# Some of the weights' low parts move from VectorE to GpSimd in stretches with urgent chains

## The chip, the cores and the metric

The kernel runs on one core of one Trainium2 chip. The metric is the device time of one execution in microseconds (us), as the median of three runs. Engines are named as the profile names them: PE is TensorE (PEld its weight loads), DVE is VectorE, ACT is ScalarE, POOL is GpSimd, SP is the engine whose queue issues most of the DMAs.

## The reference

The input is one sequence of 256 tokens of width 1024 in float32, with a memory of 256 rows. Two blocks follow each other, each of depth 2:

- Block 1, per layer: rms norm, one projection to 5120 columns (`w_in`), three branches of width 512 (attention of 8 heads with rotary positions over one causal block of 256, a gated linear recurrence called hgrn, attention to the memory), each branch times `silu(z)`, then `w_out` and the residual sum.
- Block 2, per layer: a mixer and a feed-forward net. The mixer projects to retention, a gated delta rule (names `dn`), a pooling branch and three sets of 1024 gates; `y = sum of sigmoid(gate) * (branch @ w_branch)`, then `x = x + rms_norm(y @ w_out)`. The net is `x = x + rms_norm((silu(h @ gate) * (h @ up)) @ down)` with 2816 hidden columns.

All weights are float32 and each is used once per execution.

## The kernel before

**Products.** A float32 product is made of three matmuls in the fp32r type: with x = xh + xl and w = wh + wl, `mm3` (and `chan`) does xh·wh + xh·wl + xl·wh. So each weight tile must be split before use. The weights are cut into units of 256 rows x 512 columns, stored as one tile of 128 x 1024. A unit goes through three steps, all in the class `Stream`: `_dma` loads it into a `raw` tile (5 buffers), `_split_h` casts it to `wh` on ACT, `_split_l` makes `wl = raw - wh` on DVE. The `raw` buffer comes free, for the load of five units later, when `wh` and `wl` are done. Up to 6 (wh, wl) pairs stand in pool `w`, two more in `k4` for units marked as spare.

**Use.** The 256 tokens are two tiles of 128 (t = 0, 1). `tok` takes a unit while t = 0 is worked on, with 6 matmuls for each unit and t, and uses the same units again for t = 1. `out_proj` does the last units for t = 0 and then for t = 1, so that the chain that follows t = 0 (residual, norm, transposes, next `aTh`/`aTl`) runs while PE does t = 1, and the chain of t = 1 runs while PE does t = 0 of the next phase.

**Order.** The program is written by a planner. `Order` keeps an estimated time for PE (`o.pe`) and one for each engine (`_at`; for GpSimd `Engine(self, nc.gpsimd, 150.0, 2.2)`, so 150 ns and 2.2 ns for each element of a row). Work outside the matmuls is generators (tasks) that are polled after every three matmuls; a task continues when what it waits for is ready by the estimate. Tasks spawned with `first=True` are urgent and counted in `o.urgent`: the chains at the ends of phases (`post_norm`, `residual` with the next `norm`), `branch_evac` for the `dn` branch, and the last part of the feed-forward net. At every poll `pump` may do one `_split_l`, loads, and one `_split_h`. While urgent tasks exist, a split is done only if fewer than `LEAST` = 2 split units stand ahead of the one to be taken next, or if `_room` says that the engine will be free again by 300 ns after the next urgent step is due. After the planner, the framework's scheduler orders each engine's instructions by readiness and program order in its own model; so an instruction can slip ahead of one written before it that is not ready. All of DVE's, ACT's and POOL's instructions carry line 109 (the planner's wrapper), so they are told apart by their tiles.

**Names in the rows.** `raw`, `wh`, `wl` as above; `aTh`, `aTl`: high and low part of transposed activations; `sig`, `y`: gate and sum of `branch_evac` (`sig = ps * sig`, then `y = y + sig`); `yg`, `b`, `c`, `v`, `w`, `z`, `r`, `x`, `xn`: the steps of `post_norm` and `norm` (`x = yg * r + x`, `xn = x * r * gain`); `mx`, `acc`: PSUM tiles; `rope...`, `hgrn_masks`, `lbd`, `lbe`: small work of the start.

Of the kernel before, what the change touches and what calls it, by code (L numbers as in the profile page):

```python
# [8 lines left out]
F32 = mybir.dt.float32  # L9
# [5 lines left out]
ALU = mybir.AluOpType  # L15
# [215 lines left out]
class Stream:  # L231
# [66 lines left out]
        m, k = self.units[i][3]  # L298
        return self.kb.mem_gain[m][:, 2 * k : 2 * k + 2]

    def _split_l(self):
        i = self.n_l
        w = math.prod(self.shape(i)[1:])
        h = self.h[i][:, :w]
        gain = self.gain(i)
        if gain is None:
            self.o.dve.tensor_tensor(self.l[i][:, :w], self.raw[i][:, :w], h.bitcast(F32), op=ALU.subtract)
        else:
            for k in range(2):
                c = slice(k * w // 2, (k + 1) * w // 2)  # L310
                self.o.dve.scalar_tensor_tensor(self.l[i][:, c], self.raw[i][:, c], gain[:, k : k + 1], h[:, c].bitcast(F32),
                                                op0=ALU.mult, op1=ALU.subtract)
        del self.raw[i]
        self.n_l += 1
# [9 lines left out]
    def pump(self):  # L324
        o = self.o
        if (self.n_l < self.n_h and o.when(self.h[self.n_l]) <= o.pe + o.SLACK
                and (self.n_l - self.at < self.LEAST or self._room(o.dve, 1140.0))):
            self._split_l()
        while self.n_dma < len(self.units) and self.n_dma - self.n_l < self.RAW:
            self._dma()  # L330
        least = self.n_h - self.at < self.LEAST
        if (self.n_h < min(self.n_dma, self.at + self.AHEAD) and self._can_place()
                and o.when(self.raw[self.n_h]) <= o.pe + (o.SLACK if least else -self.LANDED)
                and (least or self._room(o.act, 960.0))):
            self._split_h()
# [1574 lines left out]
```

## Time and profile before

| | |
|---|---|
| median of three runs | 1415.68 us (1414.83 to 1417.45) |
| the profiled execution's own time | 1415.08 us |
| its span, first to last instruction | 1413.3 us |
| granted clock of TensorE, mean | 0.999 |
| instructions | 20451 |
| busy: PE, PEld, DVE, ACT, POOL | 1386.1, 1166.4, 1017.3, 829.5, 26.1 us |
| DMA: bytes, mean rate | 229.06 MB, 162 GB/s |

PE's ends are modelled and its matmuls overlap, so a busy PE says only that a matmul was in work. POOL's 26.1 us lie in the first two of forty slices of the span; it does nothing after that.

### The profile page before, as it was taken

To read this page: it belongs to the slowest core of one execution; us is meant where nothing else is said; L and a number is where in the kernel's file an instruction comes from. 1 tells how busy PE (TensorE), PEld (TensorE's weight loads), DVE (VectorE), ACT (ScalarE), POOL (GpSimd) and SP (SyncE) were. 2 spreads that over 40 slices of the span, in tenths; PEclk is the share of its full clock that TensorE was granted. 3 is DMA by queue.
4 is the path that set the end of the run, shared out by engine and by line. 5 is a ranking of instruction groups with operands and counts; after the bars stand their busy time and mean duration, and the time that the engine had idled before them with its cause. 6 is when DMAs were issued, how large, how long until landed. Compare 5 with 4: busy or idle time off the path is not lost.

```text
span 1413.3 us, 20451 instructions
## 1 busy us (share of the span) xinstructions
PE 1386.1 (98%) x7608; PEld 1166.4 (83%) x7608; DVE 1017.3 (72%) x1712; ACT 829.5 (59%) x1420; POOL 26.1 (2%) x65
## 2 busy tenths in 40 slices
PE   7999999999999999999999999999999999999998
PEld 6978887887888898888877888879888887788886
DVE  6798677689897698657777655687968567665564
ACT  6676565476764466556655544565666466555453
POOL 6100000000000000000000000000000000000000
PEclk9999999999999999999999999999999999999999
DMA  8653446555345454235665566645534357465561
GB/s 279 205 162 93 136 134 213 170 152 164 120 149 177 123 184 137 80 90 178 214 190 166 190 193 190 213 138 175 150 116 123 96 187 253 120 202 185 182 189 62
DMA packets 123412, 229.06 MB, mean 162 GB/s; under 512 B 10656, under 2 KB 16560, under 8 KB 123312
## 3 DMA queue, kind: packets, MB, share of 16 engines
q1 hardware_dynamic: 123280, 227.75, 51.7%
q8 instruction: 60, 0.98, 0.3%
q14 instruction: 40, 0.33, 0.1%
q0 software_dynamic: 32, 0.00, 0.0%
HBM read 226.67 MB, written 1.05 MB: 161 GB/s over the span
## 4 chain that ended last, share of the span: by engine, by line
PE 83%; DVE 6%; DMA 4%; ACT 3%; issue 3%; SPq 0%; DVEq 0%; ACTq 0%
PE acc L137 57%; PE mx L137 22%; PE mx L147 5%; DVE wl L109 2%; ACT wh L109 2%; DMA raw<-in_w_out 1%; DMA raw<-in_ffn_gate 1%; ACT junk L109 1%; DMA mem<-in_mem 0%; DVE hlf L109 0%; DMA gqk<-in_moba_q_norm 0%; DVE hA L109 0%; ACT sg L109 0%; DMA raw<-in_w_in 0%; SPq L408 0%
## 5 line engine op out<-in xcount | busy, mean ns | idle before, releaser
L109 DVE TENSOR_TENSOR wl<-raw,wh 128x1024 fp32r<-128x1024 f32 x396 | 479.9, 1221 | 148.4 <-ACT wh L109 142.9
L109 ACT CAST wh<-raw 128x1024 fp32r<-128x1024 f32 x396 | 412.7, 1050 | 173.6 <-PE acc L137 93.6
L137 PE MATMUL acc<-wh,aTh 128*128 128x512 f32 x1232 | 494.4, 402 | 2.4 <-ACT aTh L109 2.2
L137 PE MATMUL acc<-wh,aTl 128*128 128x512 f32 x1232 | 485.0, 394 | 1.1 <-DVE aTl L109 1.1
L137 PE MATMUL acc<-wl,aTh 128*128 128x512 f32 x1232 | 485.1, 394 | 0.0
L137 PEld LDWEIGHTS acc<-wh,aTl 128*128 128x128 f32 x1232 | 232.0, 188 | 49.8 <-DVE aTl L109 2.3
L137 PEld LDWEIGHTS acc<-wh,aTh 128*128 128x128 f32 x1232 | 232.3, 189 | 49.2 <-ACT aTh L109 4.1
L137 PEld LDWEIGHTS acc<-wl,aTh 128*128 128x128 f32 x1232 | 232.3, 189 | 45.0 <-issue 1.0
L137 PE MATMUL mx<-wh,ff 128*128 128x512 f32 x352 | 111.2, 392 | 0.0
L137 PE MATMUL acc<-aTh,wh 128*128 128x256 f32 x320 | 91.1, 285 | 0.0
L137 PE MATMUL acc<-aTh,wl 128*128 128x256 f32 x320 | 90.6, 283 | 0.0
L137 PE MATMUL acc<-aTl,wh 128*128 128x256 f32 x320 | 90.5, 283 | 0.0
L137 PEld LDWEIGHTS mx<-wh,ff 128*128 128x128 f32 x352 | 65.6, 188 | 13.2
L109 ACT ACTIVATE sg<-sg 128x512 f32<-128x512 f32 (+1 forms) x120 | 73.7, 614 | 1.5
L109 ACT ACTIVATE sg<-zc 128x512 f32<-128x512 f32 (+1 forms) x60 | 36.9, 616 | 62.4 <-DVE zc L109 62.3
L137 PE MATMUL mx<-wl,ff 128*128 128x512 f32 x176 | 68.5, 389 | 0.0
L137 PEld LDWEIGHTS acc<-aTh,wh 128*128 128x128 f32 x320 | 61.3, 192 | 0.3
L137 PEld LDWEIGHTS acc<-aTh,wl 128*128 128x128 f32 x320 | 61.3, 192 | 0.2
L137 PEld LDWEIGHTS acc<-aTl,wh 128*128 128x128 f32 x320 | 61.3, 192 | 0.0
L109 DVE TENSOR_SCALAR zc<-acc 128x512 f32<-128x512 f32 (+1 forms) x48 | 31.9, 664 | 36.8 <-PE acc L137 36.8
L109 ACT CAST ff<-mx 128x256 fp32r<-128x256 f32 x44 | 14.4, 375 | 52.8 <-PE mx L147 52.8
L109 ACT CAST aTh<-mx 128x512 fp32r<-128x512 f32 x44 | 24.7, 584 | 33.2 <-PE mx L147 32.9
(317 smaller groups left out, 1654.1 us busy)
## 6 DMA issues: line engine op xcount, KB each, us to landing
raw<-in_w_in SPq DMA_DIRECT2D x200, 512.0 KB
raw<-in_ffn_down SPq DMA_DIRECT2D x44, 512.0 KB
raw<-in_w_out SPq DMA_DIRECT2D x40, 512.0 KB
raw<-in_ffn_gate SPq DMA_DIRECT2D x40, 512.0 KB
raw<-in_ffn_up SPq DMA_DIRECT2D x40, 512.0 KB
raw<-in_w_mem_kv SPq DMA_DIRECT2D x16, 512.0 KB
raw<-in_w_branch_pool SPq DMA_DIRECT2D x8, 512.0 KB
raw<-in_w_branch_ret SPq DMA_DIRECT2D x8, 512.0 KB
```

The lines of the kernel that those rows point to most:

```text
L109: r = f(out, *args, **kw)
L137: self._ns.matmul(out, lhsT, rhs, **kw)
L147: self._ns.transpose(out, x, ident)
```

## The change

When `pump` finds a low part to be made whose high part is ready, but neither fewer than two split units ahead nor room on DVE, it did nothing for that unit. Now it gives that `wl` to GpSimd, if there are urgent tasks and GpSimd's estimated time is not past PE's by more than 200 ns. The instruction is the same (`tensor_tensor`, subtract, 128 x 1024). The splits forced in `take`, those with fewer than two units ahead, and those with room stay on DVE; units with a gain never go to GpSimd, since that branch of `_split_l` doesn't use the new argument.

```diff
-    def _split_l(self):
+    def _split_l(self, engine=None):
         i = self.n_l
         w = math.prod(self.shape(i)[1:])
         h = self.h[i][:, :w]
         gain = self.gain(i)
         if gain is None:
-            self.o.dve.tensor_tensor(self.l[i][:, :w], self.raw[i][:, :w], h.bitcast(F32), op=ALU.subtract)
+            (engine or self.o.dve).tensor_tensor(self.l[i][:, :w], self.raw[i][:, :w], h.bitcast(F32), op=ALU.subtract)
...
         if (self.n_l < self.n_h and o.when(self.h[self.n_l]) <= o.pe + o.SLACK
                 and (self.n_l - self.at < self.LEAST or self._room(o.dve, 1140.0))):
             self._split_l()
+        elif self.n_l < self.n_h and o.urgent and o.when(self.h[self.n_l]) <= o.pe + o.SLACK and o.gps._at <= o.pe + o.SLACK:
+            self._split_l(o.gps)
         while self.n_dma < len(self.units) and self.n_dma - self.n_l < self.RAW:
             self._dma()
```

## Rows read from the trace of the kernel before

**Rows 1.** The page's busy times: us, share of the span, instructions.
```profile
PE 1386.1 (98%) x7608; PEld 1166.4 (83%) x7608; DVE 1017.3 (72%) x1712; ACT 829.5 (59%) x1420; POOL 26.1 (2%) x65
```

**Rows 2.** Windows: stretch, length, busy time of PE, PEld, DVE, ACT, POOL, clock, DMA.
```profile
703.40:721.30 17.90, 15.42 (x73) 11.67 (x72) 15.19 (x19) 8.91 (x12) 0.00 (x0) 1.00 0.80 259
727.00:739.00 12.00, 12.00 (x58) 9.87 (x58) 9.94 (x21) 9.46 (x20) 0.00 (x0) 1.00 0.50 138
739.00:753.00 14.00, 13.30 (x64) 10.56 (x63) 12.45 (x27) 7.27 (x17) 0.00 (x0) 1.00 0.55 183
...
917.00:932.00 15.00, 13.21 (x60) 10.11 (x59) 13.04 (x27) 12.13 (x26) 0.00 (x0) 1.00 0.53 161
...
1183.20:1201.20 18.00, 15.22 (x73) 11.62 (x72) 15.36 (x19) 9.08 (x12) 0.00 (x0) 1.00 0.85 288
...
1219.00:1233.00 14.00, 13.32 (x64) 10.57 (x63) 12.45 (x27) 7.18 (x17) 0.00 (x0) 1.00 0.57 184
...
sum 166.80, PE 158.37 PEld 126.28 DVE 140.36 ACT 93.26 POOL 0.00; mean PE 11.31 PEld 9.02 DVE 10.03 ACT 6.66 POOL 0.00
```

**Rows 3.** The same 14 windows, instructions on tile wl alone (PE, PEld, DVE).
```profile
244.00:253.00 9.00, 4.61 (x13) 2.26 (x12) 3.46 (x3) 1.00 0.40 112
...
1386.00:1396.00 10.00, 5.44 (x15) 2.64 (x14) 2.36 (x2) 1.00 0.00 0
sum 166.80, PE 79.36 PEld 38.33 DVE 58.70; mean PE 5.67 PEld 2.74 DVE 4.19
```

**Rows 4.** Timeline of DVE after the first `dn` product: start, us, instruction.
```profile
704.83 1.21 DVE L109 TENSOR_TENSOR wl<-raw,wh 128x1024 fp32r<-128x1024 f32 x1
705.96 0.68 DVE L109 TENSOR_TENSOR y<-y,sig 128x512 f32<-128x512 f32 x1
```

**Rows 5.** Timeline of PE there; in brackets idle before it and its releaser.
```profile
705.00 0.39 PE L137 MATMUL acc<-wl,aTh 128*128 128x512 f32 x1
705.23 0.39 PE L137 MATMUL acc<-wh,aTl 128*128 128x512 f32 x1
...
706.79 0.63 PE L147 MATMUL mx<-ident,y 128*128 128x128 f32 x4 [0.95 <-DVE y L109]
```

**Rows 6.** Timelines of DVE and PE in the chain behind mixer 0, t = 1.
```profile
743.71 1.21 DVE L109 TENSOR_TENSOR wl<-raw,wh 128x1024 fp32r<-128x1024 f32 x1
744.84 0.15 DVE L109 SCALAR_TENSOR_TENSOR r<-w,z 128x1 f32<-128x1 f32 x1
...
750.62 1.23 PE L147 MATMUL mx<-ident,xn 128*128 128x128 f32 x8 [0.62 <-DVE xn L109]
```

**Rows 7.** Timeline of DVE in the chain behind the first feed-forward net, t = 0.
```profile
925.25 1.23 DVE L109 TENSOR_TENSOR wl<-raw,wh 128x1024 fp32r<-128x1024 f32 x1
926.39 0.15 DVE L109 SCALAR_TENSOR_TENSOR r<-w,z 128x1 f32<-128x1 f32 x1
```

**Rows 8.** Timeline of POOL and DVE at the start.
```profile
9.99 0.25 POOL L109 TENSOR_TENSOR ropea<-ropea,ropez 128x32 f32<-128x32 f32 x1
...
10.47 1.22 DVE L109 TENSOR_TENSOR wl<-raw,wh 128x1024 fp32r<-128x1024 f32 x1 [0.58 <-ACT wh L109]
10.70 1.10 POOL L109 TENSOR_TENSOR ropea<-ropea,ropez 128x32 f32<-128x32 f32 x1
```

**Rows 9.** Timeline of POOL and DVE around a cast of masks.
```profile
48.28 1.23 DVE L109 TENSOR_TENSOR wl<-raw,wh 128x1024 fp32r<-128x1024 f32 x1 [0.22 <-ACT wh L109]
48.78 1.20 POOL L109 CAST hgrn_masks<-stage 128x512 uint8<-128x512 f32 x1 [0.46 <-DMA stage<-in_c_hgrn_masks]
...
49.64 0.35 DVE L109 TENSOR_TENSOR lbd<-cols 128x4 f32<-128x4 f32 x1
...
50.16 0.15 DVE L109 SCALAR_TENSOR_TENSOR lbe<-lbd 128x4 f32<-128x4 f32 x1
```

**Rows 10.** Groups by form on DVE, 703.4 to 753: busy us, mean ns, idle before.
```profile
L109 DVE SCALAR_TENSOR_TENSOR x<-yg,r,x 128x512 f32<-128x512 f32 x4 | 2.8, 749 | 0.1
L109 DVE SCALAR_TENSOR_TENSOR xn<-x,r,gain 128x512 f32<-128x512 f32 x4 | 2.8, 748 | 0.0
...
L109 DVE TENSOR_TENSOR y<-y,sig 128x512 f32<-128x512 f32 x4 | 2.7, 680 | 0.0
```

## The prediction

> **What bounds the kernel now.** I read the page first. PE is in work for 1386.1 of 1413.3 us [rows 1]; DVE is busy for 72% and POOL for 2%. So a change on DVE or POOL can only give or take time where PE waits. Next the windows over the 14 stretches in which urgent chains run: two tiles' chains at each end of a phase, and the evacuations of `dn` and of the last feed-forward part. There PE is in work for 158.37 of 166.80 us [rows 2]. The difference, 8.43 us, is all that faster chains could give back. It lies in five windows: 2.48 us from 703.4, 0.70 from 739, 1.79 from 917, 2.78 from 1183.2, 0.68 from 1219; the others idle for nothing. The timelines say what ends the idle time: DVE's `y` at 706.79 [rows 5] and `xn` at 750.62 [rows 6]; I found no wait for a weight among them. DVE is 84% busy there (140.36 of 166.80), and 58.70 us of that are low parts [rows 2, 3]: 50 instructions, counted over the 14 rows of that view.
>
> **What the change does, part by part.**
>
> *How many move.* A `wl` moves only if two split units stand ahead, there is no room, and its `wh` is made. The same stretches hold back the `wh` too, since ACT's room is asked in the same way, so only those made just before a chain or in a gap of it are left. All 50 is the upper end, none the lower. Of these windows' splits some are forced (fewer than two ahead) and some fall between chains where there is room, so I take half, 25 (bounds 8 and 45). POOL is empty in all of them (x0 in each row), so nothing queues on POOL but the splits themselves.
>
> *What it removes.* Each moved `wl` frees DVE for 1.13 us, the distance from a `wl` at 704.83 to the next instruction at 705.96 [rows 4]: 25 x 1.13 = 28 us of DVE. On the path that counts where PE waits behind it. At 704.83 a `wl` stands between `sig` and `y`; PE waits 0.95 us for that `y` [rows 4, 5]. Layer 1's window (1183.2) is a twin, so 1.9 us together. At 743.71 a `wl` stands ahead of `r`, which starts at 744.84, and PE waits for the `xn` that follows; with its twin I give it these windows' whole idle time, 0.70 + 0.68 = 1.4 us [rows 2, 6]. At 925.25 a `wl` holds `r` by 1.1 us [rows 7], of whose window's 1.79 us I give it 0.8. That makes 4.1 us if all the right ones move, and with half moving 2.0 us. The rest of the 8.43 us is latency of the chains themselves, which no split causes.
>
> *What it adds: the length on POOL.* The trace has no POOL instruction of this size. From below: the cast of 512 columns, begun while DVE ran a `wl`, ended at 49.98, so 0.47 us after that `wl` ended at 49.51 [rows 9]. That is 0.92 ns a column with one input, or 0.94 us for 1024. From above: the planner's own 150 + 2.2 x 1024 = 2400 ns. Two inputs at the cast's rate make 1.9 us, and with the 0.25 us that a short two-input instruction takes [rows 8] 2.1 us. I take 2.1, since a subtraction has two inputs, and keep 0.94 and 2.4 as ends.
>
> The Trainium skill, GPSIMD Engine Reference, § 3.1, gives 4497 ns for a two-input addition of 2048 float32 columns and says that VectorE is about twice as fast; my estimate from that page is 2.25 us for 1024. No run here shows it yet; by it the sum below would come out 0.6 us higher.
>
> *What it adds: the two engines hold each other up.* A POOL instruction that takes 0.25 us alone took 1.10 when it began behind a DVE `wl`, and ended just after it (11.80 against 11.69) [rows 8]. The other way round, DVE's `lbd` of 4 columns took 0.35 us, where `lbe` of the same size took 0.15, and it ended at 49.99, as the cast on POOL did [rows 9]. So while POOL works on a moved `wl`, a DVE instruction with two inputs in SBUF stands until POOL has finished. In the chains these are `y`, `x` and `xn`: from 703.4 to 753 there are 4 + 2 pairs + 2 pairs = 8 runs of them with 8.3 us, 1.04 us each [rows 10]. A POOL instruction of 2.1 us meets one with (2.1 + 1.04) x 8 / 49.6 = 0.51, and the meeting costs on average half of it, 1.05 us. So 25 x 0.51 x 1.05 = 13.4 us of chain. How much reaches PE: PE idles in 5 of the 14 windows, so chains are late in 0.36 of the cases and have some slack in the others; 13.4 x 0.36 = 4.8 us.
>
> The Trainium skill, SBUF — State Buffer, § Who interferes with whom, says the same of DVE's two-input instructions, and that one with at most one SBUF input is not held outside the two-port modes. The trace agrees as far as it goes (`lbd` above). If that rule failed and every DVE instruction were held, nearly each of the 25 would cost: 25 x 1.05 x 0.36 = 9.5 us in place of 4.8.
>
> *Loads and the order.* A `raw` buffer comes free up to 1 us later (2.1 against 1.13), and SP's queue is in order, so the loads behind a waiting one come that much later. I cost it at nothing: five buffers hide it, as long as PE finds its weights made. If that cover were gone it would be 1 us for each moved unit, 25 us at most. The extra splits also let `n_l` run ahead in the plan, so loads are issued earlier; I cost that at nothing for the same reason.
>
> **Sum.** The profiled execution took 1415.08 us (0.6 below the median): 1415.1 - 2.0 + 4.8 = 1417.9 us. It is 0.2% above, just where a measurement of this kernel can begin to tell a difference from none (about 0.2%, 2.8 us).
>
> **The rivals.**
>
> 1. *Relief wins.* PE's rows say that chains, not weights, set the idle time, and DVE's that splits stand in them. If POOL is nearer to 0.94 us, a meeting has (0.94 + 1.04) x 8 / 49.6 = 0.32 and costs 0.47 us: 25 x 0.32 x 0.47 x 0.36 = 1.4 us, against a relief of up to 4.1. That gives 1412.4 us; were all 8.43 us given back, 1406.7. Against it: most of DVE's critical steps have two SBUF inputs.
>
> 2. *Little moves, or it cancels.* With 8 moved units, the sum is 8/25 of the one above: +0.9 us, so 1416. For it: ACT's splits are held back by the same estimate, so few `wl` can be waiting. Against it: the 50 splits that do run in these windows.
>
> 3. *Much moves, with the long POOL time.* 45 units at 2.4 us: (2.4 + 1.04) x 8 / 49.6 = 0.55; 45 x 0.55 x 1.2 x 0.36 = 10.7, less 2.0: +8.7 us, so 1423.8.
>
> 4. *PE waits for weights.* A moved `wl` that first waits for a DVE `wl` takes 1.1 + 2.1 = 3.2 us. Two units ahead are 12 matmuls for t = 0, each 0.23 us after the last [rows 5], so 2.8 us: 0.4 us late. If it held for all 25, 10 us on top of the sum: 1428. It decides from the point at which a unit is fewer than 14 matmuls away. Against it: by the planner's 2.4 us it is in time, and most units stand further ahead.
>
> **How the numbers follow.** Forecast and its near cases (1414.5 to 1421): 0.40, of which half is over the 0.2% line. Rival 1 (1407 to 1412.8, with a little above): 0.28. Rival 2: 0.17. Rival 3: 0.11. Rival 4: 0.04. Slower by over 0.2% (from about 1418.5): 0.20 + 0.11 + 0.04 = 0.35. Faster by over 0.2% (under about 1412.9): 0.27 of rival 1. The rest, 0.38, is within. The range goes from 1411, inside rival 1, to 1424.5, just past rival 3; the likeliest case alone is 1414.5 to 1421.
>
> **What the profile of the changed kernel would show.** POOL has a group `wl<-raw,wh` with about 25 instructions of 2.1 us on average, longer where a DVE `wl` runs; DVE's group has as many fewer. Where POOL runs, `y`, `x` and `xn` on DVE take up to 2 us more than 0.68 or 0.75, while `sig`, `yg` and `aTl` keep their length. PE's idle time in the windows from 703.4 and 1183.2 falls by about 1 us each, and new idle time appears at chain ends that had none, as from 727. The prediction is wrong if POOL has fewer than 8 or more than 45 of them, if DVE's two-input instructions keep their length beside POOL, or if PE comes to wait for `wl`.

## The result, and the profile after

The changed kernel took 1434.01 us (median of four runs, 1432.63 to 1438.61), the kernel before 1415.26 in runs beside it: a ratio of 1.0138, 95% interval [1.0124, 1.0152]. It is 18.75 us slower, and lies 9.5 us above the end of the predicted range. The profiled execution was the longest of the four: own time 1438.61, span 1436.8, mean granted clock 0.991 (before 0.999). What the trace accounts for below is thus some 5 us more than the median shows.

The page's busy times after, to be held against [rows 1]:

```profile
PE 1394.1 (97%) x7608; PEld 1174.2 (82%) x7608; DVE 1022.4 (71%) x1691; ACT 830.3 (58%) x1420; POOL 81.8 (6%) x86
```

DVE has 21 instructions fewer, POOL 21 more, and still DVE is busy for 5.1 us longer: what is left on it got longer. Take PE's busy time from the span and the loss falls into two parts. PE is out of work for 42.7 us (1436.8 − 1394.1) in place of 27.2, 15.5 us more; and the same 7608 matmuls are in work for 8.0 us longer. Together that is the 23.5 us by which the two spans differ.

First the idle part. PE's waits, the two longest rows for DVE: what waited, for what, us in total, times, longest. First of before, then of after:

```profile
PE mx L147 <- DVE y L109: 6.4, 6, 1.4
...
PE mx L147 <- DVE xn L109: 3.9, 5, 1.4
```

```profile
PE mx L147 <- DVE y L109: 14.7, 8, 4.5
PE mx L147 <- DVE xn L109: 12.7, 6, 2.9
```

17.1 us more, in 14 waits for 11: above all the waits grew longer. No row of PE names a weight (`wl` or `wh`), and two of its weight loads waited for a `wl` of DVE, 0.6 us in all; so the moved low parts themselves were in time. The tile view of `wl` says how long they took (ns, minimum / median / maximum):

```profile
L109 DVE TENSOR_TENSOR wl<-raw,wh x375: 1192/1224/3418, 7.8 to 1411.5; 128x1024 fp32r<-128x1024 f32 x188
L109 POOL TENSOR_TENSOR wl<-raw,wh x21: 2348/2475/3474, 244.8 to 1234.2; 128x1024 fp32r<-128x1024 f32 x21
```

So POOL takes 2.35 to 2.40 us when it has the way free (eight of the 21, in the timelines), and a DVE `wl` can now take 3.4 us.

What happens where PE waits is best seen behind the first `dn` product, the stretch of [rows 4] and [rows 5]. Timelines of DVE, then POOL, ACT, PE and SP, and last the same two DVE steps before:

```profile
707.21 2.19 DVE L109 TENSOR_TENSOR y<-y,sig 128x512 f32<-128x512 f32 x1
709.32 0.68 DVE L109 TENSOR_TENSOR sig<-acc,sig 128x512 f32<-128x512 f32 x1
710.03 2.17 DVE L109 TENSOR_TENSOR y<-y,sig 128x512 f32<-128x512 f32 x1
...
717.11 1.23 DVE L109 TENSOR_TENSOR wl<-raw,wh 128x1024 fp32r<-128x1024 f32 x1 [2.00 <-ACT wh L109]
718.25 2.83 DVE L109 TENSOR_TENSOR y<-y,sig 128x512 f32<-128x512 f32 x1
...
706.08 10.75 POOL L109 TENSOR_TENSOR wl<-raw,wh 128x1024 fp32r<-128x1024 f32 x4 [249.50 <-ACT wh L109]
718.09 2.44 POOL L109 TENSOR_TENSOR wl<-raw,wh 128x1024 fp32r<-128x1024 f32 x1 [1.27 <-ACT wh L109]
...
716.02 2.94 ACT L109 CAST wh<-raw 128x1024 fp32r<-128x1024 f32 x3 [2.42 <-DMA raw<-in_ffn_gate]
...
721.23 1.09 PE L147 MATMUL mx<-ident,y 128*128 128x128 f32 x4 [4.13 <-DVE y L109]
...
711.68 3.17 SPq L254 DMA_DIRECT2D raw<-in_ffn_gate  x2
```

```profile
713.08 0.68 DVE L109 TENSOR_TENSOR y<-y,sig 128x512 f32<-128x512 f32 x1
714.98 1.23 DVE L109 TENSOR_TENSOR wl<-raw,wh 128x1024 fp32r<-128x1024 f32 x1 [1.23 <-ACT wh L109]
```

Four low parts stand back to back on POOL, and each of the first two `y` takes 2.2 us where it took 0.68. Each ends 0.55 us after one of the POOL instructions (709.40 for 708.85, 712.21 for 711.66), and the POOL instruction that begins meanwhile takes 2.84 us: the `y` stands until POOL lets it go, then POOL stands until the `y` is done. `sig`, whose `acc` is in PSUM, keeps its 0.68 under the same POOL work. The third `y` shows both ways in which the change delays a chain. Its `sig` was done at 715.10, but ahead of it in DVE's queue stands a `wl` that waits 2.00 us for its `wh`, and ACT's `wh` waits for a load of `in_ffn_gate`. These loads begin at 711.68, as POOL's second low part ends and lets go of its `raw` buffer; before they began at 706.07. Yet against the chain the load is there hardly later: ACT starts on it 8.8 us after the first `y` began, and 7.9 before (713.90, 705.96 [rows 4]). What is new is the order: before, the third `y` went ahead of the `wl` that waits for this load. Then POOL's next low part, begun 0.16 us earlier, holds the `y` for 2.1 us more. PE waits 4.13 us. Layer 1's twin, at 1211.74, waits 4.45.

The chain behind mixer 0, t = 1, the stretch of [rows 6]:

```profile
741.30 2.04 DVE L109 SCALAR_TENSOR_TENSOR w<-y,v 128x1 f32<-128x1 f32 x1 [0.93 <-ACT y L109]
743.26 0.14 DVE L109 TENSOR_SCALAR z<-y 128x1 f32<-128x1 f32 x1
743.44 2.21 DVE L109 SCALAR_TENSOR_TENSOR r<-w,z 128x1 f32<-128x1 f32 x1
...
740.92 4.71 POOL L109 TENSOR_TENSOR wl<-raw,wh 128x1024 fp32r<-128x1024 f32 x2 [20.38 <-ACT wh L109]
...
746.58 1.29 PE L147 MATMUL mx<-ident,xn 128*128 128x128 f32 x8 [2.89 <-DVE xn L109]
```

`w` and `r` work on one column, and take 2.04 and 2.21 us, 1.8 and 2.05 more than alone; the first two `y` above, of 512 columns, lost 1.5 each. A short instruction can lose as much as a long one.

Over DVE's whole timeline, 16 instructions that touch one of the 21 took over 0.3 us longer than the median of their form: six `y`, four `w`, three `wl`, two `r`, one `x`. Together they are 27.5 us longer, 1.72 us each. The 24 instructions of `sig`, `aTl`, `x<-mx`, `b`, `c`, `v` and `z` that touch one have their usual length. So have ten with two inputs in SBUF (seven `wl`, two `xn`, one `x`), and each of these had begun before the POOL instruction that it meets.

Now the 8 us of slower matmuls. Windows after, as in [rows 2]: the granted clock is the figure ahead of the DMA share.

```profile
263.80:267.20 3.40, 3.40 (x12) 2.72 (x10) 1.61 (x3) 0.89 (x2) 0.00 (x0) 0.50 0.36 136
717.10:721.20 4.10, 0.00 (x0) 0.00 (x1) 4.09 (x3) 1.86 (x2) 2.44 (x1) 1.00 0.94 340
721.20:724.60 3.40, 3.37 (x10) 2.90 (x11) 2.91 (x4) 0.59 (x1) 0.00 (x0) 0.50 0.77 261
724.60:728.00 3.40, 3.40 (x18) 2.76 (x17) 0.69 (x1) 0.59 (x1) 0.00 (x0) 1.00 0.53 163
939.70:943.10 3.40, 3.40 (x12) 2.58 (x11) 3.31 (x7) 2.73 (x7) 0.00 (x0) 0.50 0.86 232
1209.30:1216.10 6.80, 4.36 (x13) 3.62 (x14) 5.32 (x5) 0.76 (x2) 1.74 (x1) 0.50 0.81 236
1236.60:1243.40 6.80, 5.88 (x18) 5.04 (x19) 5.57 (x7) 3.12 (x5) 0.00 (x0) 0.50 0.66 196
```

PE stood still from 717.1 to 721.2; in the 3.4 us after that the granted clock is 0.50 (1.2 GHz), and the row counts 10 matmuls, where the next 3.4 us at full clock (2.4 GHz) have 18. Matmuls of 512 columns start 0.43 us apart at the lower clock and 0.23 at the higher. There are five such stretches, each at one of the new stalls, 23.8 us in all, and 38 matmuls of 512 columns start in them: an estimate of 38 x 0.2 = 7.6 us, which is about the 8. Before, the windows from 700 to 728 and from 1180 to 1250 had a clock of 1.00.

### The profile page after: what moved, and what is told of

Same layout as the page of the kernel before. It is cut to its first block, busy times and chain, and to the rows that moved or that the text cites. A ratio compares the mean times of both kernels' runs of the same rounds, so it can differ in the third digit from the quotient of the medians.

```text
span 1436.8 us, 20462 instructions
## 1 busy us (share of the span) xinstructions
PE 1394.1 (97%) x7608; PEld 1174.2 (82%) x7608; DVE 1022.4 (71%) x1691; ACT 830.3 (58%) x1420; POOL 81.8 (6%) x86
## 3 DMA queue, kind: packets, MB, share of 16 engines
HBM read 226.67 MB, written 1.05 MB: 158 GB/s over the span
## 4 chain that ended last, share of the span: by engine, by line
PE 84%; DVE 6%; ACT 3%; DMA 3%; issue 3%; POOL 0%; DVEq 0%; SPq 0%; ACTq 0%; POOLq 0%
PE acc L137 58%; PE mx L137 21%; PE mx L147 5%; DVE wl L109 2%; ACT wh L109 2%; DMA raw<-in_w_out 2%; DMA raw<-in_w_in 1%; DMA raw<-in_ffn_gate 1%; DVE w L109 0%; DVE y L109 0%; POOL wl L109 0%; DVE r L109 0%; DVE x L109 0%; ACT junk L109 0%; DVE hlf L109 0%
## 5 line engine op out<-in xcount | busy, mean ns | idle before, releaser
L109 DVE TENSOR_TENSOR wl<-raw,wh 128x1024 fp32r<-128x1024 f32 x375 | 459.9, 1234 | 146.3 <-ACT wh L109 141.6
L109 POOL TENSOR_TENSOR wl<-raw,wh 128x1024 fp32r<-128x1024 f32 x21 | 54.3, 2600 | 1127.9 <-ACT wh L109 759.4
```

Of the source, the lines that this page charges most:

```text
L109: r = f(out, *args, **kw)
```

## The experiments

The two theories at the outset: **held steps** (POOL's long read keeps DVE's two-input steps standing, and PE waits for those) against **order** (the change alters when low parts are made and loads are issued, and that costs the time whoever does the work).

| kernel | us | ratio to before [95%] |
|---|---|---|
| the same low parts at the same polls, on DVE | 1418.92 | 1.0024 [1.0013, 1.0036] |
| POOL reads 32 columns only | 1418.55 | 1.0021 [1.0006, 1.0035] |
| POOL in four pieces | 1427.77 | 1.0086 [1.0071, 1.0101] |
| `w` and `r` in a form with one full input | 1432.21 | 1.0121 [1.0106, 1.0136] |
| POOL in calm stretches only | 1425.12 | 1.0078 [1.0061, 1.0095] |
| POOL in evacuations only | 1423.69 | 1.0064 [1.0049, 1.0079] |
| POOL in chains at phase ends only | 1422.30 | 1.0055 [1.0040, 1.0070] |
| before, six raw buffers | 1421.68 | 1.0050 [1.0035, 1.0065] |
| before, low parts pinned | 1415.51 | 1.0008 [0.9998, 1.0017] |
| changed, low parts pinned | 1432.32 | 1.0121 [1.0105, 1.0136] |
| short read, low parts pinned | 1418.63 | 1.0019 [1.0009, 1.0030] |
| before, pinned in evacuations only | 1410.66 | 0.9973 [0.9963, 0.9983] |

**The same low parts on DVE.** POOL's estimated time goes on as if it had done them, so that about the same splits are let through.

```diff
-            self._split_l(o.gps)
+            at = max(o.gps._at, o.pe, o.ready[self.h[self.n_l].name]) + 2403.0
+            self._split_l()
+            o.gps._at = at
```

> The splits that the change gives to GpSimd are made at the same points of the plan, but on VectorE. If the two engines hold each other up (the first theory), nothing of the loss is left: within 3 us of the kernel before, 1412 to 1418 us. If the new points in the plan, and the order of instructions that follows from them, are what costs (the rival), the loss stays for the larger part: 1425 us or more.

1418.92 us: 3.5 us over before, some 15 under the changed kernel, and 0.9 above the range that held steps gave. Most of the loss hangs on the work being on POOL. Where the 3.5 us lie is not shown: the profiled execution is the fastest of the ten, 1415.41 us, level with before, and the longer ones have a lower mean granted clock (0.998 down to 0.994). Its trace shows that the order can cost: PE waits 4.33 us at 928.12, behind the first feed-forward net, where DVE makes six low parts between the first `x` and `xn`, with the chain's small steps among them.

**A short read.** POOL subtracts 32 columns and sets the other 992 to zero, with the planner's times as in the changed kernel. So most of each moved low part is left out.

```diff
-            (engine or self.o.dve).tensor_tensor(self.l[i][:, :w], self.raw[i][:, :w], h.bitcast(F32), op=ALU.subtract)
...
+                engine.tensor_tensor(self.l[i][:, :32], self.raw[i][:, :32], h[:, :32].bitcast(F32), op=ALU.subtract)
+                engine.memset(self.l[i][:, 32:w].bitcast(F32), 0.0)
...
```

> GpSimd subtracts only the first 32 columns of a moved split and fills the other 992 with zeros, which reads nothing; the rest of those low parts is left out of the computation. Same points in the plan, same waits, about as long on GpSimd. If it is GpSimd's reading that holds VectorE's two-input instructions, a hold lasts 0.25 us and the loss goes: 1411 to 1418 us. If the order costs, or any work on GpSimd, 1430 us or more.

1418.55 us, 0.55 above what held steps gave (1411 to 1418); the order theory's 1430 is out. POOL's groups and the stall that stayed:

```profile
L109 POOL MEMSET wl<- 128x992 f32 x21 | 19.5, 928 | 714.1 <-PE acc L137 512.5 <-PE mx L137 195.2 <-issue 6.4
L109 POOL TENSOR_TENSOR wl<-raw,wh 128x32 fp32r<-128x32 f32 x21 | 7.5, 357 | 428.2 <-PE mx L137 369.1 <-DVE c L109 41.1 <-ACT wh L109 17.7
```

```profile
713.22 1.23 DVE L109 TENSOR_TENSOR wl<-raw,wh 128x1024 fp32r<-128x1024 f32 x1 [3.69 <-ACT wh L109]
714.36 0.74 DVE L109 TENSOR_TENSOR y<-y,sig 128x512 f32<-128x512 f32 x1
...
715.25 0.63 PE L147 MATMUL mx<-ident,y 128*128 128x128 f32 x4 [3.94 <-DVE y L109]
```

POOL is busy here for 27 us with `wl`, half of the changed kernel's time, yet no DVE instruction beside it is longer by over 0.3 us: writing zeros holds nothing. What stays is DVE's queue: a `wl` that waits for a load stands ahead of a `y` that could go. This run also takes away POOL's longer hold of the `raw` buffer, since each low part is done in 1.3 us for 2.6, so by itself it doesn't part the two. But the stall that stayed does not come of that hold: here the first load of `in_ffn_gate` is issued at 704.33, 0.8 us after the first `y` began, and ACT has it only at 712.14.

**Four pieces.** The same subtraction in four instructions of 256 columns.

```diff
-            (engine or self.o.dve).tensor_tensor(self.l[i][:, :w], self.raw[i][:, :w], h.bitcast(F32), op=ALU.subtract)
+            e, n = engine or self.o.dve, 4 if engine else 1
+            for k in range(n):
+                c = slice(k * w // n, (k + 1) * w // n)
+                e.tensor_tensor(self.l[i][:, c], self.raw[i][:, c], h[:, c].bitcast(F32), op=ALU.subtract)
```

> Each moved split is made in four subtractions of 256 columns on GpSimd, some 0.65 us each. If GpSimd holds VectorE for the length of one instruction and lets it in between two, a held step loses 0.3 to 0.7 us in place of 1 to 2.2: 1417 to 1425 us. If the hold goes on over consecutive instructions, or if the order costs, 1430 us or more.

1427.77 us: 6.2 less than whole, and between the two expectations. In its chain behind mixer 0 the timelines have

```profile
735.93 0.60 DVE L109 SCALAR_TENSOR_TENSOR r<-w,z 128x1 f32<-128x1 f32 x1
736.57 2.34 DVE L109 SCALAR_TENSOR_TENSOR xn<-x,r,gain 128x512 f32<-128x512 f32 x2
...
735.77 6.87 POOL L109 TENSOR_TENSOR wl<-raw,wh 128x256 fp32r<-128x256 f32 x7
```

`r` waits out one piece and then goes: the hold is for one instruction, and is let go between two. All holds sum to 8.1 us here, over 19 moved low parts (27.5 over 21 with the whole instruction). POOL is on each low part for longer than in the changed kernel, 3.5 us for 2.6, so the `raw` buffer comes free later still; that the time falls all the same speaks for the holds as the cause. The gain is smaller than theirs, since the stall behind a waiting `wl` (4.4 us at 714.95) is as in the kernel above.

**One-input form of `w` and `r`.** They become `tensor_scalar` with per-row scalars; `xn` and the rest stay.

```diff
-        self.dve.scalar_tensor_tensor(w, y, v, y, op0=ALU.mult, op1=ALU.mult)
+        self.dve.tensor_scalar(w, y, v, y, op0=ALU.mult, op1=ALU.mult)
...
-        self.dve.scalar_tensor_tensor(r, w, 3.0, z, op0=ALU.add, op1=ALU.mult)
+        self.dve.tensor_scalar(r, w, 3.0, z, op0=ALU.add, op1=ALU.mult)
```

> As the changed kernel, but w and r in the norm, instructions of one column with two tensors in SBUF as inputs, are written with one tensor and per-row scalars. If only a second tensor input is held, w and r run through beside GpSimd (0.2 us in place of up to 2.2) and the ends of phases gain 4 to 8 us: 1425 to 1431 us. If every instruction that reads SBUF is held, or if the wait only goes over to x and xn, no change: 1432 to 1436 us.

1432.21 us, hardly faster, as the second case expected, and the timelines say why:

```profile
737.50 0.27 DVE L109 TENSOR_SCALAR w<-y,v 128x1 f32<-128x1 f32 x1 [0.93 <-ACT y L109]
737.68 0.14 DVE L109 TENSOR_SCALAR z<-y 128x1 f32<-128x1 f32 x1
737.86 0.22 DVE L109 TENSOR_SCALAR r<-w,z 128x1 f32<-128x1 f32 x1
738.12 4.71 DVE L109 SCALAR_TENSOR_TENSOR xn<-x,r,gain 128x512 f32<-128x512 f32 x2
...
737.11 5.17 POOL L109 TENSOR_TENSOR wl<-raw,wh 128x1024 fp32r<-128x1024 f32 x2 [20.17 <-ACT wh L109]
```

In this form `w` and `r` are not held (0.27 and 0.22 under POOL's work). The chain merely arrives sooner at its next two-input step, and is held there.

**Calm stretches only.** Every eighteenth unit goes to POOL if three or more split units stand ahead and no urgent task exists; the branch for urgent stretches is gone.

```diff
-            self._split_l()
-        elif self.n_l < self.n_h and o.urgent and o.when(self.h[self.n_l]) <= o.pe + o.SLACK and o.gps._at <= o.pe + o.SLACK:
-            self._split_l(o.gps)
+            self._split_l(o.gps if not o.urgent and self.n_l % 18 == 17 and self.n_l - self.at >= 3 and o.gps._at <= o.pe + o.SLACK else None)
```

> About as many low parts (14) go to GpSimd, but only while no urgent chain stands: every eighteenth unit, three or more split units ahead. Theory (GpSimd's reading holds VectorE's two-input steps, and that costs only where PE waits for those steps): no step that PE waits for is near, so 1413 to 1418.5 us, PE's waits for y and xn as before. Rival (each low part on GpSimd costs its 1.3 us of extra length wherever it stands, through later weights and loads): 14 x 0.9 us, 1425 or more.

1425.12 us: a miss, 6.6 above my theory's range and at the rival's figure. But the rival's mechanism isn't there: PE waits 0.2 us in all for a `wl`. The time is in steps that the planner doesn't call urgent:

```profile
192.68 2.86 DVE L109 TENSOR_TENSOR y<-on,sz 128x512 f32<-128x512 f32 x1
...
192.31 2.68 POOL L109 TENSOR_TENSOR wl<-raw,wh 128x1024 fp32r<-128x1024 f32 x1 [139.58 <-ACT wh L109]
...
195.60 0.78 PE L147 MATMUL mx<-ident,y 128*128 128x128 f32 x4 [1.95 <-DVE y L109]
```

It is the same at 1249.98, where `f<-zc,sg` takes 2.45 us and PE waits 1.78. Eight held instructions with two inputs lose 12.6 us, and a stretch at half clock follows the first (196.0, 3.4 us). A ninth has one input:

```profile
517.82 2.25 DVE L109 TENSOR_SCALAR zc<-conv 128x512 f32<-128x512 f32 x1
```

The other eleven of these take 0.42 us; this one lost 1.8, and it ended 0.29 us after a POOL low part that had begun ahead of it (517.09, 2.70 us). So not every one-input step goes free: this one reads SBUF and takes 0.42 us for 512 columns, where `zc<-acc`, from PSUM, takes 0.69 and wasn't held. My theory of the cause held in the main; that calm stretches have no step that PE waits for was wrong.

**Evacuations only, and chains at phase ends only.** `o.urgent` in the new branch is replaced by one kind of urgent task each:

```diff
-        elif self.n_l < self.n_h and o.urgent and ...
+        elif self.n_l < self.n_h and any(t[3] and not t[1] for t in o.tasks) and ...
```

> GpSimd takes low parts only while a dn evacuation or the last feed-forward part is urgent (10 of them); the chains at ends of phases keep VectorE alone. The stalls of the changed kernel that PE's y waits end are here, 8.3 us more than before, with half-clock spells behind two of them: 1423 to 1428 us, and its loss and that of the next kernel add up to some 18.6 us. Rival (one shared cause, the plan's shift, makes the loss in either): both near 1419 or both near 1430.

The other has `t[3] and t[1]`.

> GpSimd takes low parts only while a chain at the end of a phase is urgent (11 of them). The stalls that PE's xn waits end are here, 8.8 us more than before, with half-clock spells behind two or three of them: 1422 to 1428 us, PE's waits for y as before (6.4 us) and those for xn near 12.7. Rival as for the kernel before it: both near 1419 or both near 1430.

1423.69 and 1422.30 us, with 10 and 11 moved low parts. Over before these are 8.8 and 7.5 us, 16.3 in sum, against 18.75 for the whole change with its 21. PE's waits split roughly as foreseen: for `y` 14.4 us and for `xn` 4.3 in the first, 8.0 and 10.6 in the second. So the loss goes with the moved low parts, each half where it stands, and not with one shift of the whole plan. The 2.5 us between are within what the two intervals leave open (some 2 us each). For each moved low part the calm stretches paid 0.73 us, the evacuations 0.88, the phase ends 0.68.

**Six raw buffers, in the kernel before.** `RAW` 6 in place of 5, and 20 `k2` buffers for 22 to make room.

> The kernel before with six raw buffers in place of five (two of the 22 small k2 buffers given up for the room): the control for the changed kernel with six. If loads that come late set any of the idle time before, 1 to 3 us faster than before; if not, within 3 us of it (1412 to 1418).

1421.68 us, slower than either case expected, with new stalls of 3.8 us at 933.15 and 3.3 at 405.38. It was meant as the control for the changed kernel with six; with a control this far off that was not run, and what POOL's longer hold of `raw` costs by itself stays open. It does show, with the run on DVE, how easily another order costs this kernel 3 to 7 us.

**Pinned low parts.** While an urgent task exists, a DVE `wl` keeps its place behind what was written before it on DVE; the scheduler can no longer let it slip ahead of a chain step that isn't ready in its model.

```diff
-            self.o.dve.tensor_tensor(self.l[i][:, :w], self.raw[i][:, :w], h.bitcast(F32), op=ALU.subtract)
+            r = self.o.dve.tensor_tensor(self.l[i][:, :w], self.raw[i][:, :w], h.bitcast(F32), op=ALU.subtract)
+            if self.o.urgent:
+                self.kb.tc.keep_in_program_order(r)
```

> The kernel before, but a low part that VectorE makes while an urgent chain stands keeps its place in the program: it can't slip ahead of a chain step that was written before it. Nothing goes to GpSimd. Theory (low parts that slipped ahead of a chain's steps set the idle time of the urgent stretches): the 8.4 us of idle there fall, 1409 to 1413 us. Rival (weights then come later than PE takes them): PE waits for wl or for steps of the chain behind it, 1418 or more.

> The changed kernel with the same pin. If the 4.3 us stalls of the dn stretches (from 715 and from 1203) come of a low part that slipped between sig and y and waited there for a late load, they fall under 2 us each and the half-clock spells behind them go: 1423 to 1428 us, the rest being steps held by GpSimd. Rival (the late load itself stops PE, whatever stands in VectorE's queue): PE waits there for a weight instead, 1431 or more.

> The kernel with GpSimd's short read (32 of 1024 columns subtracted, the rest set to zero, so those low parts are left out) with the same pin. With neither GpSimd's long reading nor low parts slipping ahead, the theory leaves no loss: 1408 to 1414 us. Rival (late loads stop PE by themselves): still near 1418.5.

In the changed kernel the pin does what was expected in the stretch of the timelines above: from 703 to 722 PE waits 2.4 us for `y` (5.4 unpinned), and no wait for `y` in the whole run is over 1.2 us. Yet the whole takes 1432.32 us, not the 1423 to 1428 expected, for PE now waits 5.5 us for `wl` (at 750.41, 942.22 and 1241.13, behind ends of phases), and 3.7 us for `xn` at 1228.66, behind a `w` and an `r` that POOL holds for 2.35 and 2.20 us. In the kernel before, pinned, 1415.51, the waits show the same exchange:

```profile
PE acc L137 <- DVE wl L109: 6.2, 5, 2.2
...
PE mx L147 <- DVE y L109: 4.7, 4, 1.7
...
PE mx L147 <- DVE xn L109: 1.9, 2, 1.3
```

The chains gain 3.7 us (10.3 before) and PE loses 6.2 for low parts made too late. Neither theory was right in full; both mechanisms are there and cancel. The short read with the pin, 1418.63, is a miss too: the theory had 1408 to 1414, the rival 1418.5, and PE waits 5.2 us there for `wl`. With the pin, the long read against the short one still costs 13.7 us (1432.32 against 1418.63), as it does without it (1434.01 against 1418.55: 15.5).

**Pinned in evacuations only.** The long ones of those five waits for `wl` (2.2 us the longest) stand at the phase ends, so there the order is left as it was. The condition of the pin is `any(t[3] and not t[1] for t in self.o.tasks)`.

> The kernel before with the pin only while a dn evacuation or the last feed-forward part is urgent, where the pinned kernel's waits for y fell without a wait for a weight in their place; the chains at ends of phases, where PE then waited 1.85 to 2.4 us for weights, keep their order. Theory: y's waits fall by 1 to 2 us, 1412.5 to 1414.5 us, about 0.1% faster than before. Rival (what the chain gains, the weights behind it lose here too): 1415 to 1417 us.

1410.66 us against 1415.23, faster than both kernels and by more than expected. PE's waits, with no row for `wl` left:

```profile
PE mx L147 <- DVE xn L109: 4.4, 6, 1.3
PE mx L147 <- DVE y L109: 2.9, 3, 1.2
```

## Why the prediction was wrong

**Right.** The place (PE's waits for `y` and `xn` at the chains), the mechanism (two-input DVE steps and POOL's read hold each other, steps with an input in PSUM and the chains' one-column steps with one input go free), the count (21 moved for 25) and that PE would not wait for a moved `wl`. The length was put too low: 2.1 us, where POOL took 2.35 to 2.40 when it wasn't itself held; that is the planner's own 2.4, the upper end. The estimate of 2.25 us from the Trainium skill, GPSIMD Engine Reference, § 3.1 (4497 ns for 2048 columns) was nearer than mine, and still too low.

**The failed step: the holds, sized at 13.4 us; they were 27.5.** Two choices made it small. The list of steps that can be held was `y`, `x` and `xn`; `w`, `r` and DVE's own `wl`, which have two inputs in SBUF as well, were left out without a reason. They are 9 of the 16 held. And a meeting was priced at half a POOL instruction, 1.05 us, as if the two met at random. They don't: POOL's splits follow one another (four from 706.08, 10.75 us), so a step that is let go at the end of one is followed by a step that finds the next one just begun. Measured: 1.72 us each.

By itself this does not carry the time out of the range: 27.5 x 0.36 = 9.9 us in place of 4.8 makes 1423.0. The three terms below do the rest.

The Trainium skill, SBUF — State Buffer, § Who interferes with whom, says that the order of issue decides which of the two stands, and that an instruction that only writes on GpSimd holds no two-input step. The runs agree with both: ten steps that had begun first kept their length, `y` begun second took 2.19 us beside POOL's subtraction, and none was held beside the 21 zero fills of 928 ns.

**The share of 0.36 that reaches PE.** It took the chains for late in 5 of 14 windows only. Against the same low parts on DVE, POOL costs 15.1 us (1434.01 − 1418.92), so 0.55 of the 27.5 (an estimate: the first is a difference of medians, the second from the longest execution). A part of this is the half clock, which no step of the prediction had: 23.8 us of PE at 0.50.

**Loads and the order at nothing.** The cover named, that PE finds its weights made, held: PE never waited for one. What broke was a queue that I had not looked at: a `wl` that waits for a load keeps a chain step behind it waiting, too. In the short read, where holds are gone, this is the 3.94 us at 715.25. All new orderings together are the 3.5 and 3.2 us that the run on DVE and the short read have over before; what each part is worth can't be told apart, as the pinned kernels show, where the waits only changed place.

**The relief of 2.0 us.** It showed in part, and was lost again. Behind the first `dn` product no low part of DVE stands between the first `sig` and `y` any more, and PE waits 0.47 us for this `y` in place of 0.95, and 0.79 for the second in place of 1.03; the third then costs 4.13. In layer 1 the first costs 2.51 in place of 1.22. That relief was there to be had, the last kernel shows, which gets 4.6 us by order alone and moves nothing to POOL.

In the prediction's own terms: holds of 27.5 us add 5.1 us to the forecast's 2.8, the share of 0.55 another 5.2, the relief that was not kept 2.0, and the order 3.5. That makes 18.6 of the 18.75. The share is what was left over, so the sum proves nothing; it says what each step weighed.

## What to carry to other kernels

Before moving work to GpSimd, list every two-input SBUF instruction of VectorE near it, single-column ones too, and charge each more than half a GpSimd instruction: here a held step lost 1.72 us beside one of 2.4. Calm stretches were no cheaper for each moved low part than urgent ones; a planner's "not urgent" is no proof that nothing waits. When an early instruction in an in-order queue can wait for a load, look at who stands behind it; to keep the written order at a few such places gave 4.6 us here, where the second engine cost 18.75.

## What the runs showed of the hardware that was not expected

- A one-column instruction (`w`, 0.22 us alone) stands for 2.04 us beside POOL; written with per-row scalars it takes 0.27 there.
- A one-input step can be held too: `zc<-conv`, 0.42 us alone, took 2.25 beside POOL in the run on calm stretches.
- A stall's length alone did not decide whether half clock followed: after 2.14 us idle before 262.82 the clock was 0.50 from 263.8, after 2.89 us before 746.58 it was 1.00 from 746.6 to 753.4. What told the two apart is open.
